# Low-rank up-projections with value and remainder stacked in one tile: two matmuls for three, and one for three

## The chip, the cores and the metric

The kernel runs on one core of one Trainium2 chip. The metric is the device time of one execution in microseconds (us): the median of the runs of a kernel. Engine names are those of the profile: PE (TensorE matmul), DVE (VectorE), ACT (ScalarE), POOL (GpSimd), SP (the queue that issues most DMAs).

## The reference

One encoder layer is applied to two batches of 512 tokens with width 1024. It has two branches on the normalised input, a recurrent one (RWKV7, run in both directions) and an attention one (MLA), then a gated feed-forward block. The part that the change touches feeds the recurrence: the decays, the rates and the output gate each come from a low-rank product.

```python
DECAY_LORA = 64; ICLR_LORA = 64; GATE_LORA = 160; A_WIDTH = 512
def decay(lora, up, base):
    wl = -jax.nn.softplus(-(base + jnp.tanh(lora) @ up)) - 0.5
    return jnp.exp(-jnp.exp(wl))
def iclr(lora, up, base):
    return jax.nn.sigmoid(base + lora @ up)
wf, wb = decay(pwf, w2[0], w0[0]), decay(pwb, w2[1], w0[1])   # forward, backward
af, ab = iclr(paf, a2[0], a0[0]), iclr(pab, a2[1], a0[1])
g = jax.nn.sigmoid(pg) @ g2
```

So four products have an inner size of 64, and the gate has one of 160.

## The kernel before

All large products keep float32 accuracy with a rounded matmul type: every operand is split into a rounded value "hi" and a remainder "lo" (`split`: ACT casts, DVE subtracts), and `mm3` adds three matmuls, hi by hi, hi by lo and lo by hi, into one PSUM tile.

The program has these stages. First the two inputs are normalised and transposed. Then `lora_phase` projects the input onto the low-rank columns (`proj` of tiles 4, 5, 6 and 3: "pj_w", "pj_a", "pj_g", "pj_x", 48 matmuls each of 512 columns, or their equal in halves), shifts them in time (`shifted`), applies tanh, and splits the results: `lw` (both decays: rows 0 to 63 forward, 64 to 127 backward), `la` (both rates), `lg` (128 of the gate's 160 rows) and `lx` (its last 32, in rows 64 to 95). After that a loop over four pairs of heads p and two batches b makes 40 PSUM tiles: four tiles "lu" (i = 0, 1 decays, 2, 3 rates) and one tile "lug" (the gate). A "lu" tile takes one `mm3`; its weights `w2` are zero in the 64 rows of the other direction. ACT applies tanh to it (tile "lut"), POOL scales it, and a DMA stores it to DRAM (`rwkv_in`). A "lug" tile takes two `mm3`, DVE copies it, and a DMA stores it. The PSUM tiles of this loop rotate over two banks (tag "mg"), the "lut" tiles over four buffers.

A scheduler of the framework sets each engine's order in this stage from its own time estimates, so that matmuls of later projections ("pj_rkv", "pj_mla") stand between the "lu" groups as long as there are any. From the next stage on (`drive`) the order of PE is written by the program: six threads (the recurrence's `state`, its `post`, `merge` and `prep`, the filler projections with the attention, and `combine`) are taken in turn by a model of PE time, in which the constants `L1`, `L2`, `L3`, `YS`, `YQ`, `YK` are the delays after which a thread may go on. `YS` stands ahead of a unit's recurrence, `L2` inside it; `YQ` and `YK` stand behind the query and key projections of the attention. The order of the other engines there is again the scheduler's. In the attention, "sc" are the scores of one block of queries, "mx" their maxima, "pr" the softmax (ACT exponential, DVE scaling), "pt" its transpose on PE, "pT" the copy of it by ACT, and "pav" the product with the values.

The feed-forward block and its down projection ("dx", "dy" in 2x2 blocks with split operands "dA", "dB", "dS", "dT") end the program.

Of the kernel before, what the change touches and what calls it, by code (L numbers as in the profile page):

```python
# [11 lines left out]
F32R = mybir.dt.float32r  # L12
# [6 lines left out]
P = 128  # L19
NB = 2  # L20
S = 512
# [18 lines left out]
ALAG = 2  # L40
NSTART = 27
L1 = 0.7
L2 = 0.9
L3 = 1.0
TL = 40
SLACK = 1.4
# [18 lines left out]
YO1 = 1.3  # L65
YO2 = 2.11
YO3 = 3.44
YS = 0.5
YQ = 2.6
YK = 1.4  # L70
OFFS = 200000, 150000, 120000, 100000, 0, 0
JP = NFF // 2
NRH = 10
# [31 lines left out]
def trunk(ctx, tc, outs, x, w_in, w2, g2, w_uq, w_ukk, w_ukv, w_oab, w_out, w_gu, w_down,  # L105
          cols, fng, ident, te, to, mask2, reset, blk64, blk2):
    nc = tc.nc
    out_p, out_s = outs

    def pool(stack, name, bufs=1, **kw):  # L110
        return stack.enter_context(tc.tile_pool(name=name, bufs=bufs, reuse_waits="tile", **kw))
# [11 lines left out]
    def mm(out, lhsT, rhs, start=True, stop=True, **kw):  # L123
        n = math.prod(rhs.shape[1:]) * (1 if rhs.dtype == F32R else 4) / 2400
        pin(nc.tensor.matmul(out, lhsT, rhs, start=start, stop=stop, **kw), n if out.shape[0] > 64 else n / 2)  # L125
# [5 lines left out]
    def split(hi, lo, src, eng=None):  # L131
        nc.scalar.copy(hi, src)  # L132
        (eng or nc.vector).tensor_sub(lo, src, hi)  # L133

    def mm3(out, whi, wlo, xhi, xlo, start=True, stop=True, **kw):
        mm(out, whi, xhi, start=start, stop=False, **kw)
        yield 0
        mm(out, whi, xlo, start=False, stop=False, **kw)
        yield 0
        mm(out, wlo, xhi, start=False, stop=stop, **kw)  # L140
        yield 0
# [88 lines left out]
    def mg(name):  # L230
        return psf.tile([P, S], F32, tag="mg", bufs=2, name=name)
# [52 lines left out]
    def proj(ti, name):  # L284
        res = [pf(f"pj_{name}{b}") for b in range(NB)]
        wt = []
        for q in range(2):
            raw = wp.tile([P, 4 * P], F32, tag="wraw", bufs=2, name=f"wraw_{name}{q}")
            nc.sync.dma_start(raw, w_in[ti][:, q * 512:(q + 1) * 512])
            hi = wp.tile([P, 4 * P], F32R, tag="whi", bufs=2, name=f"whi_{name}{q}")  # L290
            lo = wp.tile([P, 4 * P], F32R, tag="wlo", bufs=2, name=f"wlo_{name}{q}")
            split(hi, lo, raw)
            wt.append((hi, lo))
        n = 2 if ti in HALVES else 1
        for b in range(NB):
            for q in range(n):
                qs = slice(q * S // n, (q + 1) * S // n)
                for k in range(KD):
                    hi, lo = wt[k // 4]
                    ks = slice(k % 4 * P, (k % 4 + 1) * P)  # L300
                    yield from mm3(res[b][:, qs], hi[:, ks], lo[:, ks], h_hi[b][:, k, qs], h_lo[b][:, k, qs],
                                   start=(k == 0), stop=(k == KD - 1))
        return res

    def sh(name):
        return wp.tile([P, S], F32, tag="sh", bufs=2, name=name)
# [97 lines left out]
    def lora_phase():  # L404
        with ExitStack() as sl:
            lp = pool(sl, "lora")
            lw = [[lp.tile([P, S], F32R, name=f"lw{b}{i}") for i in range(2)] for b in range(NB)]
            la = [[lp.tile([P, S], F32R, name=f"la{b}{i}") for i in range(2)] for b in range(NB)]
            lg = [[lp.tile([P, S], F32R, name=f"lg{b}{i}") for i in range(2)] for b in range(NB)]
            lx = [[lp.tile([P, S], F32R, name=f"lx{b}{i}") for i in range(2)] for b in range(NB)]  # L410
            tosb = lp.tile([64, S], F32, name="tosb")
            nc.sync.dma_start(tosb, to[0:64])
            for b, ps in enumerate((yield from proj(4, "w"))):
                t = sh(f"shw{b}")
                shifted(t, ps, T_W)
                nc.scalar.activation(t, t, AF.Tanh)
                split(*lw[b], t)
            for b, ps in enumerate((yield from proj(5, "a"))):
                t = sh(f"sha{b}")
                shifted(t, ps, T_A)  # L420
                split(*la[b], t)
            for b, ps in enumerate((yield from proj(6, "g"))):
                t = sh(f"shg{b}")
                shifted(t, ps, T_G)
                nc.scalar.activation(t, t, AF.Tanh, scale=0.5)
                nc.vector.tensor_scalar(t, t, 0.5, 0.5, op0=ALU.mult, op1=ALU.add)
                split(*lg[b], t)
            for b, ps in enumerate((yield from proj(3, "x"))):
                t = sh(f"shx{b}")
                nc.vector.memset(t, 0.0)  # L430
                r = slice(64, 96)
                shifted(t, ps, T_X, r)
                nc.scalar.activation(t[r], t[r], AF.Tanh, scale=0.5)
                nc.vector.tensor_scalar(t[r], t[r], 0.5, 0.5, op0=ALU.mult, op1=ALU.add)
                split(*lx[b], t)
                ta, tb = sh(f"kra{b}")[0:32], sh(f"krb{b}")[0:32]
                nc.vector.tensor_mul(ta, ps[0:32], tosb[0:32])
                nc.vector.tensor_mul(tb, ps[32:64], tosb[32:64])
                nc.vector.tensor_add(ta, ta, tb)
                nc.sync.dma_start(kr_d[b][0:32], ta)  # L440
                nc.sync.dma_start(kr_d[b][32:64], ta)
            w2hi = lp.tile([P, 4, S], F32R, name="w2hi")
            w2lo = lp.tile([P, 4, S], F32R, name="w2lo")
            g2hi = lp.tile([P, 2, S], F32R, name="g2hi")
            g2lo = lp.tile([P, 2, S], F32R, name="g2lo")
            for i in range(4):
                t = lp.tile([P, S], F32, tag="raw", bufs=2, name=f"w2raw{i}")
                nc.sync.dma_start(t, w2[i])
                split(w2hi[:, i], w2lo[:, i], t)
            for i in range(2):  # L450
                t = lp.tile([P, S], F32, tag="raw", bufs=2, name=f"g2raw{i}")
                nc.sync.dma_start(t, g2[i])
                split(g2hi[:, i], g2lo[:, i], t)
            for p in range(NPAIR):
                for b in range(NB):
                    sl_p = slice(p * P, (p + 1) * P)
                    for i in range(4):
                        src = lw if i < 2 else la
                        ps = mg(f"lu{b}{p}{i}")
                        yield from mm3(ps, w2hi[:, i, sl_p], w2lo[:, i, sl_p], src[b][0], src[b][1])  # L460
                        t = lp.tile([P, S], F32, tag="lut", bufs=4, name=f"lut{b}{p}{i}")
                        dst = t[:, ::-1] if i % 2 else t
                        hcol = half[:, i * 4 + p:i * 4 + p + 1]
                        nc.scalar.activation(dst, ps, AF.Tanh, scale=0.5, bias=hcol)  # L464
                        f = -0.5 * KAPPA if i < 2 else 0.5
                        nc.gpsimd.tensor_scalar(t, t, f, f, op0=ALU.mult, op1=ALU.add)  # L466
                        nc.sync.dma_start(rwkv_in[b][p][:, 3 + i], t)
                    ps = mg(f"lug{b}{p}")
                    yield from mm3(ps, g2hi[:, 0, sl_p], g2lo[:, 0, sl_p], lg[b][0], lg[b][1], stop=False)
                    yield from mm3(ps, g2hi[:, 1, sl_p], g2lo[:, 1, sl_p], lx[b][0], lx[b][1], start=False)  # L470
                    t = lp.tile([P, S], F32, tag="lut", bufs=4, name=f"lugt{b}{p}")
                    nc.vector.tensor_copy(t, ps)
                    nc.sync.dma_start(rwkv_in[b][p][:, 7], t)
        yield from rkv_tiles(0)
# [53 lines left out]
    def attn_q(ap, b, hd, qn, tab):  # L528
# [13 lines left out]
        split(qh, ql, qf, QLE(nc))  # L542
        return qh, ql, pe["now"] + pe["cost"] + YQ

    def attention(ap, meanwhile):
# [45 lines left out]
        for (b, hd), (b1, hd1) in zip(heads, heads[1:] + [(NB, 0)]):  # L591
# [7 lines left out]
            for qb in range(4):  # L599
# [12 lines left out]
                if b1 < NB:  # L612
# [4 lines left out]
                    if qb == 3 and e == 1:  # L617
                        if hd1 == 0:
                            kt = attn_kr(ap, b1)
                        attn_kt(kt, kps)  # L620
                        q = (q[0], q[1], max(q[2], pe["now"] + YK))
                while len(pending) > ALAG:
# [63 lines left out]
    class Unit:  # L686
# [195 lines left out]
        def state(self):  # L882
# [20 lines left out]
            for c in range(NCH):  # L903
# [25 lines left out]
                nc.vector.tensor_copy(svb[HB, :, c], s2[HB])  # L929
                yield L2  # L930
                if not last:
# [49 lines left out]
    def state_thread():  # L981
        for i in range(NU):
            yield has("merge", i)
            yield has("prep", i)
            yield YS
            yield from units[i].state()
# [622 lines left out]
def layout(i):  # L1609
    f = np.float32  # L1610
    a = {k: np.asarray(v) for k, v in i.items()}
    r = {}
# [18 lines left out]
    r["w_in"] = wt.reshape(len(cols), P, KD * P)  # L1631
    w2 = np.zeros((4, P, 512), f)
    for d in range(2):
        w2[d, d * 64:(d + 1) * 64] = a["decay_w2"][0, d]
        w2[2 + d, d * 64:(d + 1) * 64] = a["iclr_a2"][0, d]
    r["w2"] = w2
    g2 = np.zeros((2, P, 512), f)
    g2[0] = a["gate_g2"][0, :128]
    g2[1, 64:96] = a["gate_g2"][0, 128:]
    r["g2"] = g2  # L1640
    uq = a["w_uq"][0].reshape(2, P, 8, 96)
    even = np.concatenate([np.arange(96), 80 + np.arange(16), 64 + np.arange(16)])
# [76 lines left out]
```

## Time and profile before

| | |
|---|---|
| median of 3 runs | 1831.26 us (1829.73 to 1834.43) |
| profiled execution | 1833.27 us |
| its span, first to last instruction | 1831.4 us |
| mean granted PE clock | 0.979 |
| PE busy | 1725.9 us (94%) |
| DVE, ACT, POOL busy | 1116.1, 771.4, 640.4 us |

The profiled execution stands 2.0 us above the median, of which the span leaves out 1.9 us. A busy share says how long an engine had an instruction under way; since matmuls overlap, the length of a PE stretch is read from the distance between starts, not from the duration of a matmul. The chain of work that ended last is followed back from the end of the program; a wait in it moves the end, a wait outside does not.

### The profile page before, as it was taken

To read this page: it belongs to the slowest core of one execution; us is meant where nothing else is said; L and a number is where in the kernel's file an instruction comes from. 1 tells how busy PE (TensorE), PEld (TensorE's weight loads), DVE (VectorE), ACT (ScalarE), POOL (GpSimd) and SP (SyncE) were. 2 spreads that over 40 slices of the span, in tenths; PEclk is the share of its full clock that TensorE was granted. 3 is DMA by queue.
4 is the path that set the end of the run, shared out by engine and by line. 5 is a ranking of instruction groups with operands and counts; after the bars stand their busy time and mean duration, and the time that the engine had idled before them with its cause. 6 is when DMAs were issued, how large, how long until landed. Compare 5 with 4: busy or idle time off the path is not lost.

```text
span 1831.4 us, 30995 instructions
## 1 busy us (share of the span) xinstructions
PE 1725.9 (94%) x11676; PEld 1357.8 (74%) x11676; DVE 1116.1 (61%) x1957; ACT 771.4 (42%) x1496; POOL 640.4 (35%) x992
## 2 busy tenths in 40 slices
PE   6999989999999998899989999699999999989997
PEld 6887767777777775565656979578888888868886
DVE  6633555635355455877776556865655556588757
ACT  5434343333344335666663233333333333335445
POOL 3012345363644627161012124853434333200006
PEclk8999989999999998999999999899999999999999
DMA  4354433434333334212067651022222222374442
GB/s 165 121 175 162 124 106 89 119 80 126 106 107 117 84 109 117 60 34 58 28 240 229 194 175 35 24 81 93 97 96 90 93 81 90 100 270 128 131 139 92
DMA packets 185333, 208.97 MB, mean 114 GB/s; under 512 B 102816, under 2 KB 114464, under 8 KB 185184
## 3 DMA queue, kind: packets, MB, share of 16 engines
q1 hardware_dynamic: 184320, 205.48, 35.9%
q8 instruction: 92, 1.51, 0.3%
q10 hardware_dynamic: 720, 0.98, 0.2%
q0 software_dynamic: 144, 0.52, 0.1%
q14 instruction: 57, 0.47, 0.1%
HBM read 147.70 MB, written 59.24 MB: 113 GB/s over the span
## 4 chain that ended last, share of the span: by engine, by line
PE 67%; DVE 10%; DMA 8%; POOL 7%; issue 4%; ACT 3%; SPq 1%; POOLq 0%; DVEq 0%; ACTq 0%
PE pgC L125 10%; PE pgB L125 6%; PE pgA L125 6%; PE pj_gt L125 6%; PE pj_rkv L125 5%; PE dx L125 5%; PE dy L125 3%; POOL el L841 2%; POOL lt L839 2%; PE pab L125 2%; PE s L125 2%; PE pav L125 2%; PE pj_mla L125 2%; DMA wor<-in_w_out 2%; PE gx L125 2%
## 5 line engine op out<-in xcount | busy, mean ns | idle before, releaser
L839 POOL TENSOR_TENSOR lt<-lane,el 128x126 f32<-128x126 f32 (+22 forms) x248 | 95.6, 386 | 40.8 <-DMA lane<-nt_d 22.3
L841 POOL TENSOR_TENSOR el<-el,lt 128x126 f32<-128x126 f32 (+22 forms) x248 | 98.5, 397 | 19.1
L125 PE MATMUL pab<-yo,wab 128*128 128x512 f32 x384 | 94.8, 400 | 8.3 <-ACT yo L132 3.7
L125 PE MATMUL pj_gt<-h_lo,whi_gt 128*128 128x512 f32 x240 | 99.5, 415 | 0.0
L125 PE MATMUL pj_gt<-h_hi,whi_gt 128*128 128x512 f32 x240 | 99.0, 413 | 0.0
L125 PE MATMUL pj_gt<-h_hi,wlo_gt 128*128 128x512 f32 x240 | 98.4, 410 | 0.5 <-DVE wlo_gt L133 0.5
L125 PE MATMUL pwo<-woh,m 128*128 128x256 f32 x512 | 93.6, 283 | 0.0
L125 PEld LDWEIGHTS pab<-yo,wab 128*128 128x128 f32 x384 | 71.0, 190 | 29.1 <-DVE wab L133 4.8
L1209 POOL TENSOR_TENSOR s<-uraw 128x512 f32<-128x512 f32 x22 | 29.2, 1328 | 153.3 <-DMA uraw<-in_w_gu 153.3
L125 PEld LDWEIGHTS pwo<-woh,m 128*128 128x128 f32 x512 | 80.3, 192 | 0.3
L125 PE MATMUL pj_rkv<-h_hi,whi_rkv 128*128 128x512 f32 x192 | 79.4, 414 | 0.0
L125 PE MATMUL pj_rkv<-h_hi,wlo_rkv 128*128 128x512 f32 x192 | 79.0, 415 | 0.0
L125 PE MATMUL pj_rkv<-h_lo,whi_rkv 128*128 128x512 f32 x192 | 78.4, 409 | 0.0
L125 PE MATMUL pwo<-wol,m 128*128 128x256 f32 x256 | 72.4, 284 | 0.5 <-DVE wol L133 0.5
L1588 POOL TENSOR_TENSOR x<-x,dp 128x512 f32<-128x512 f32 x4 | 6.3, 1590 | 176.9 <-DVE x L1587 176.9
L1277 DVE TENSOR_TENSOR p<-p,pgC 128x512 f32<-128x512 f32 x22 | 15.1, 687 | 86.9 <-PE pgC L125 86.9
L1056 POOL TENSOR_TENSOR g<-g 128x512 f32<-128x512 f32 x16 | 24.5, 1533 | 97.1 <-DVE g L1054 85.9
L928 ACT COPY sva<-s 64x128 f32<-64x128 f32 x64 | 16.5, 257 | 95.6 <-PE s L125 86.3
L466 POOL TENSOR_SCALAR lut<-lut 128x512 f32<-128x512 f32 x32 | 20.5, 642 | 98.4 <-ACT lut L464 98.1
L929 DVE COPY svb<-s 64x128 f32<-64x128 f32 x64 | 18.9, 295 | 57.6 <-ACT sva L928 34.8
L125 PEld LDWEIGHTS pj_gt<-h_hi,wlo_gt 128*128 128x128 f32 x240 | 45.1, 188 | 9.4 <-DVE wlo_gt L133 1.2
L125 PEld LDWEIGHTS pj_gt<-h_hi,whi_gt 128*128 128x128 f32 x240 | 45.1, 188 | 8.8
(1559 smaller groups left out, 5570.2 us busy)
## 6 DMA issues: line engine op xcount, KB each, us to landing
graw<-in_w_gu SPq DMA_DIRECT2D x22, 512.0 KB, 3.5
uraw<-in_w_gu SPq DMA_DIRECT2D x22, 512.0 KB, 3.5
a_d<-a SPq DMA_DIRECT2D x21, 512.0 KB, 3.2
w<-in_w_down SPq DMA_DIRECT2D x42, 256.0 KB, 4.3
x<-in_x SPq DMA_DIRECT2D x16, 512.0 KB, 7.8
rwkv_in<-lut SPq DMA_DIRECT2D x32, 256.0 KB, 2.0
gate_d<-gtt SPq DMA_DIRECT2D x32, 256.0 KB, 2.4
wab<-in_w_oab SPq DMA_DIRECT2D x32, 256.0 KB, 3.5
```

The costliest lines, as they stand in the source:

```text
L125: pin(nc.tensor.matmul(out, lhsT, rhs, start=start, stop=stop, **kw), n if out.shape[0] > 64 else n / 2)
L466: nc.gpsimd.tensor_scalar(t, t, f, f, op0=ALU.mult, op1=ALU.add)
L839: eng.tensor_mul(lv, lane[:, s, s + 1:].unsqueeze(1).to_broadcast([P, m_, n]), el[:, 0:m_, s].unsqueeze(2).to_broadcast([P, m_, n]))
L841: eng.tensor_add(ev, ev, lv)
L928: nc.scalar.copy(sva[HA, :, c], s2[HA])
L929: nc.vector.tensor_copy(svb[HB, :, c], s2[HB])
L1056: nc.gpsimd.tensor_add(g_[:, 0], g_[:, 0], g_[:, 1])
L1209: vg(ES[min(j, 1)]).tensor_add(s1, a21, a22)
L1277: nc.vector.tensor_add(p1, p1, x_)
L1588: nc.gpsimd.tensor_add(xs(1, t, 1), xs(1, t, 1), p5[t])
```

## The change

1. `lw` and `la`: for each direction one tile is made in which the 64 rows of this direction hold the rounded value, and the other 64 rows hold its remainder (`stacked`). The weights `w2` hold the direction's 64 rows twice. One matmul with the rounded weights then gives hi by hi and hi by lo at once, and a second one with the weights' remainder gives lo by (hi + lo). Each "lu" tile takes two matmuls.
2. `lx`: one tile per batch holds the last 32 gate rows three times, as value, value and remainder, and a tile `g2x` the weights as remainder, value, value, so that one matmul takes the place of three.
3. Three matmuls per "lug" tile for `lg` stay as they were.
4. The splitting takes more instructions of fewer rows: per `lw` or `la` tile two casts and two subtractions of 64 rows, per `lx` three casts and one subtraction of 32 rows.
5. Four delays of the PE model: `L2` 0.9 to 1.04, `YS` 0.5 to 0.41, `YQ` 2.6 to 2, `YK` 1.4 to 1.72.

```diff
-L2 = 0.9
+L2 = 1.04
-YS = 0.5
-YQ = 2.6
-YK = 1.4
+YS = 0.41
+YQ = 2
+YK = 1.72
...
+            top, bot = slice(0, 64), slice(64, 128)
+
+            def stacked(dst, t):
+                for d, (own, other) in enumerate(((top, bot), (bot, top))):
+                    nc.scalar.copy(dst[d][own], t[own])
+                    nc.vector.tensor_sub(dst[d][other], t[own], dst[d][own])
...
-                split(*lw[b], t)
+                stacked(lw[b], t)
...
-                split(*la[b], t)
+                stacked(la[b], t)
...
-                split(*lx[b], t)
+                for rows, own in ((slice(0, 32), slice(0, 32)), (r, r), (slice(32, 64), r)):
+                    nc.scalar.copy(lx[b][rows], t[own])
+                nc.vector.tensor_sub(lx[b][96:128], t[r], lx[b][r])
...
-                split(g2hi[:, i], g2lo[:, i], t)
+                if i == 0:
+                    split(g2hi, g2lo, t)
+                else:
+                    nc.scalar.copy(g2x[bot], t[bot])
+                    nc.scalar.copy(g2x[0:32], t[0:32])
+                    nc.vector.tensor_sub(g2x[32:64], t[64:96], g2x[64:96])
...
-                        yield from mm3(ps, w2hi[:, i, sl_p], w2lo[:, i, sl_p], src[b][0], src[b][1])
+                        mm(ps, w2hi[:, i, sl_p], src[b][i % 2], stop=False)
+                        yield 0
+                        mm(ps, w2lo[:, i, sl_p], src[b][i % 2], start=False)
+                        yield 0
...
-                    yield from mm3(ps, g2hi[:, 0, sl_p], g2lo[:, 0, sl_p], lg[b][0], lg[b][1], stop=False)
-                    yield from mm3(ps, g2hi[:, 1, sl_p], g2lo[:, 1, sl_p], lx[b][0], lx[b][1], start=False)
+                    yield from mm3(ps, g2hi[:, sl_p], g2lo[:, sl_p], lg[b][0], lg[b][1], stop=False)
+                    mm(ps, g2x[:, sl_p], lx[b], start=False)
+                    yield 0
...
-        w2[d, d * 64:(d + 1) * 64] = a["decay_w2"][0, d]
-        w2[2 + d, d * 64:(d + 1) * 64] = a["iclr_a2"][0, d]
+        w2[d] = np.tile(a["decay_w2"][0, d], (2, 1))
+        w2[2 + d] = np.tile(a["iclr_a2"][0, d], (2, 1))
...
-    g2[1, 64:96] = a["gate_g2"][0, 128:]
+    g2[1, 64:] = np.tile(a["gate_g2"][0, 128:], (2, 1))
```

In the built program PE has 48 rows of matmuls fewer (32 of "lu", 16 net of "lug"), DVE 4 instructions more, ACT 9 more (in 7 more rows); POOL's order is the same. Ahead of "lug02" (batch 0, pair 2), 28 of the 48 are taken out between projections; from its first row to the end of "lug13", with no projection between them, 20. Numbers in the names below: batch, pair, product; the number behind the underscore only tells tiles apart. PE, the tile "lu120" and its successor before:

```order
L125 MATMUL lu120_1007<-lw10_383,w2hi_769 128x512
L125 MATMUL lu120_1007<-lw11_384,w2hi_769 128x512
L125 MATMUL lu120_1007<-lw10_383,w2lo_770 128x512
L125 MATMUL lu121_1015<-lw10_383,w2hi_769 128x512
L125 MATMUL lu121_1015<-lw11_384,w2hi_769 128x512
L125 MATMUL lu121_1015<-lw10_383,w2lo_770 128x512
```

and PE at the same place with the change, with the end of "lug02" ahead of it:

```order
L125 MATMUL lug02_981<-lx0_393,g2x_783 128x512
L125 MATMUL lu120_989<-lw10_383,w2hi_779 128x512
L125 MATMUL lu120_989<-lw10_383,w2lo_780 128x512
L125 MATMUL lu121_996<-lw11_384,w2hi_779 128x512
L125 MATMUL lu121_996<-lw11_384,w2lo_780 128x512
```

Nothing moves against its neighbours there; a row is gone from each tile, and the two directions now read tiles of their own.

The second place is ACT ahead of the second "rkv" projection, whose rounded weights are "whi_rkv010". "kt000" reads "a000", a rate of the first unit that has gone through DRAM: "lut002", POOL, a store, and a load. ACT before, from "lut002" on:

```order
L464 ACTIVATE lut002_817<-lu002_813,half_65 128x512
L132 CAST lg00_389<-shg0_659 128x512
L464 ACTIVATE lut003_825<-lu003_821,half_65 128x512
L425 ACTIVATE shg1_667<-shg1_667 128x512
L132 CAST lg10_391<-shg1_667 128x512
L743 ACTIVATE kt000_1577<-a000_1567,oka_66,col_60 128x512
```

and ACT with the change:

```order
L482 ACTIVATE lut002_826<-lu002_823,half_65 128x512
L443 CAST lx0_393<-shx0_743 32x512 x2
L482 ACTIVATE lut003_833<-lu003_830,half_65 128x512
L309 ACTIVATE shx1_761<-pj_x1_682,c0_64 32x512
L443 CAST lx1_394<-shx1_761 32x512
L762 ACTIVATE kt000_1541<-a000_1531,oka_66,col_60 128x512
L440 ACTIVATE shx1_761<-shx1_761 32x512
L482 ACTIVATE lut100_848<-lu100_845,half_65 128x512
L443 CAST lx1_394<-shx1_761 32x512 x2
L132 CAST whi_rkv010_1174<-wraw_rkv010_1172 128x512
```

"lu002" and "lu003" now stand on PE behind the whole of "pj_x" (before: ahead of it), so "lut002" and "kt000" come later; before, "whi_rkv010" stood ten rows behind "kt000", now four.

The third place is DVE in the attention, where "pr013" (batch 0, head 1, last block of queries) is scaled beside the preparation of the last recurrence unit ("kra130", "bt130", "kt130", "c113", "bt131", "kt131"). DVE before:

```order
L605 TENSOR_REDUCE mx020_8332<-sc020_8315 128x1
L961 TENSOR_TENSOR os12_8145<-os12_8145,rbp_gn12_8324 128x512
L758 TENSOR_TENSOR kra130_8426<-nkk13_8283,pp130_8394 128x8x64
L759 TENSOR_TENSOR kra130_8426<-rkv13_8006,pp130_8394 128x8x64
L609 RECIPROCAL mx013_8264<-mx013_8264 128x1
L741 TENSOR_TENSOR bt130_8398<-bt130_8398,c013_8389 128x512
L745 TENSOR_TENSOR kt130_8401<-kt130_8401,c013_8389 128x512
L606 TENSOR_SCALAR mx020_8332<-mx020_8332 128x1
L740 SCALAR_TENSOR_TENSOR bt131_8414<-nkk13_8283,a131_8407 128x512
L605 TENSOR_REDUCE mx021_8349<-sc021_8345 128x1
L744 TENSOR_TENSOR kt131_8417<-kt131_8417,rkv13_8006 128x512
L734 SCALAR_TENSOR_TENSOR c113_8405<-rst_361,c113_8405 128x512
```

with "pr013" as the next row; and with the change:

```order
L624 TENSOR_REDUCE mx020_8296<-sc020_8279 128x1
L628 RECIPROCAL mx013_8228<-mx013_8228 128x1
L980 TENSOR_TENSOR os12_8111<-os12_8111,rbp_gn12_8288 128x512
L759 SCALAR_TENSOR_TENSOR bt131_8378<-nkk13_8247,a131_8371 128x512
L624 TENSOR_REDUCE mx021_8313<-sc021_8309 128x1
L763 TENSOR_TENSOR kt131_8381<-kt131_8381,rkv13_7972 128x512
L625 TENSOR_SCALAR mx020_8296<-mx020_8296 128x1
L629 TENSOR_SCALAR pr013_8231<-pr013_8231,mx013_8228 128x512
L777 TENSOR_TENSOR kra130_8390<-nkk13_8247,pp130_8358 128x8x64
L778 TENSOR_TENSOR kra130_8390<-rkv13_7972,pp130_8358 128x8x64
L760 TENSOR_TENSOR bt130_8362<-bt130_8362,c013_8353 128x512
L764 TENSOR_TENSOR kt130_8365<-kt130_8365,c013_8353 128x512
```

Five instructions, the two "kra130", "bt130", "kt130" and the scan "c113", stand behind "pr013" instead of ahead of it; a little earlier "kt011", which frees a PSUM tile, has passed "bo13" and the scan "c013". On ACT, eight instructions stand between the exponential of "pr013" and the copy "pT01" that follows the transpose of "pr013" and "kt131": "kt131" first, then "pp130", "pT01" of the block before, "c013", "os12", "e030", the exponential of "pr020" and the cast "wqh05".

Elsewhere the order differs in small ways: the matmuls "sc00x", "qps01" and "vps00" at the attention's start stand up to six rows earlier between the recurrence's rows, and in the down projection "dx" and "dy" groups and their DVE splits trade places by a few rows.

More of the change, by code (lines that the diff above doesn't have):

```diff
@@ L409, in lora_phase @@
             lg = [[lp.tile([P, S], F32R, name=f"lg{b}{i}") for i in range(2)] for b in range(NB)]
-            lx = [[lp.tile([P, S], F32R, name=f"lx{b}{i}") for i in range(2)] for b in range(NB)]
+            lx = [lp.tile([P, S], F32R, name=f"lx{b}") for b in range(NB)]
             tosb = lp.tile([64, S], F32, name="tosb")
@@ L443, in lora_phase @@
             w2lo = lp.tile([P, 4, S], F32R, name="w2lo")
-            g2hi = lp.tile([P, 2, S], F32R, name="g2hi")
-            g2lo = lp.tile([P, 2, S], F32R, name="g2lo")
+            g2hi = lp.tile([P, S], F32R, name="g2hi")
+            g2lo = lp.tile([P, S], F32R, name="g2lo")
+            g2x = lp.tile([P, S], F32R, name="g2x")
             for i in range(4):
```

## The prediction

> **What bounds the kernel now.** I read the page's first part, then the chain, then the stretches of the stage that changes, then its instructions in order of time.
>
> ```profile
> PE 1725.9 (94%) x11676; PEld 1357.8 (74%) x11676; DVE 1116.1 (61%) x1957; ACT 771.4 (42%) x1496; POOL 640.4 (35%) x992
> PE 67%; DVE 10%; DMA 8%; POOL 7%; issue 4%; ACT 3%; SPq 1%; POOLq 0%; DVEq 0%; ACTq 0%
> ```
>
> PE is busy nearly all the time and is two thirds of the chain, so matmuls taken away can shorten the program, if PE is the bound where they stand. The stretches say where it is (start and end, length, then busy time and instructions of PE, PEld, DVE, ACT and POOL, the granted clock, the DMA share, GB/s):
>
> ```profile
> 53.00:141.65 88.65, 88.65 (x390) 72.78 (x388) 40.55 (x62) 39.25 (x64) 13.03 (x20) 1.00 0.46 149
> 141.65:158.00 16.35, 15.50 (x61) 10.42 (x60) 2.08 (x3) 8.27 (x12) 7.26 (x12) 1.00 0.55 210
> ```
>
> The first stretch runs from the first "lu" matmul to the start of "lug02". PE never waits there: 390 matmuls in 88.65 us, 0.2273 us each, since the scheduler has projections to put between the "lu" tiles. The second is what is left of the loop when they have run out: "lug02" to the end of "lug13", 60 matmuls, which would take 13.6 us at 0.2273 and take 16.35. Here PE waits for the two PSUM banks. Its rhythm in order of time (start, duration, engine, line):
>
> ```profile
> 141.65 0.62 PE L125 MATMUL lug<-lg,g2hi 128*128 128x512 f32 x2
> 142.80 0.40 PE L125 MATMUL lug<-lx,g2lo 128*128 128x512 f32 x1
> 143.28 0.69 DVE L472 COPY lugt<-lug 128x512 f32<-128x512 f32 x1 [5.81 <-PE lug L125]
> 143.49 0.39 PE L125 MATMUL lu<-lw,w2lo 128*128 128x512 f32 x1
> 143.96 0.69 ACT L464 ACTIVATE lut<-lu,half 128x512 f32<-128x512 f32 x1 [5.07 <-issue]
> 144.03 0.73 PE L125 MATMUL lu<-lw,w2hi 128*128 128x512 f32 x2 [0.16 <-DVE lugt L472]
> 144.84 0.63 PE L125 MATMUL lu<-la,w2hi 128*128 128x512 f32 x2
> 146.63 0.64 PE L125 MATMUL lug<-lg,g2hi 128*128 128x512 f32 x2
> 156.60 0.64 PE L125 MATMUL lug<-lg,g2hi 128*128 128x512 f32 x2
> ```
>
> One group of five tiles takes 4.98 us (141.65 to 146.63; three of them end at 156.60), against 4.09 us of matmuls.
>
> **The change part by part.** First the 28 matmuls taken out of the dense stretch: 28 x 0.2273 = 6.4 us, on the path, as PE is the bound there. [...] The trace's 0.2273 is used.
>
> Second, the tail. A bank is held from the first matmul into it until ACT has read it. From the rows: the last matmul's start to ACT's start 0.47 us (143.49 to 143.96), ACT 0.69, and 0.19 until the next matmul there (144.65 to 144.84); for "lug" 0.48, DVE 0.69 and 0.06 (142.80, 143.28, 143.97, 144.03). Two banks alternate. With three and six matmuls these give 4.98 us a group, as measured. With two and four, from "lug" at 0: "lu" i = 0 starts at 0.91 in the other bank, ACT reads it from 1.61 to 2.30; i = 1 at 1.91; i = 2 at 2.49, but ACT is busy with i = 1 until 3.30; i = 3 at 3.49; the next "lug" at 4.18. So ACT and the banks bound it, not PE's 2.73 us. A second bound are the four "lut" buffers:
>
> ```profile
> L464 ACT ACTIVATE lut<-lu,half x32: 670/688/698, 56.5 to 156.8; 128x512 f32<-128x512 f32 x32
> L466 POOL TENSOR_SCALAR lut<-lut x32: 617/620/910, 57.3 to 157.6; 128x512 f32<-128x512 f32 x32
> DMA to landing us min/median/max: 2.0/2.0/5.9
> ```
>
> A buffer is held for 0.69 + 0.62 + 2.0 us and some 0.1 of issue, 3.4 us; five tiles over four buffers, the "lugt" one shorter by POOL's time, need 4.1 to 4.2 us a group too. Walking through both bounds together I get 4.17 and 4.34 in turn, 4.25 on the mean. The tail is three groups and one "lug": saved 3 x (4.98 - 4.25) + 2 x 0.23 = 2.7 us. The ends: 2.9 with the banks alone, 0.5 if a landing takes 2.6 us, at which the buffers ask for the old 5 us.
>
> Third, the added splits. An instruction of half the rows costs about as much as one of all:
>
> ```profile
> 54.92 0.62 ACT L132 CAST la<-sha 128x512 fp32r<-128x512 f32 x1
> 744.27 0.57 ACT L525 CAST kt<-kps 64x512 fp32r<-64x512 f32 x1
> 55.66 0.69 DVE L133 TENSOR_TENSOR la<-sha,la 128x512 fp32r<-128x512 f32 x1
> 746.26 0.67 DVE L526 TENSOR_TENSOR kt<-kps,kt 64x512 fp32r<-64x512 f32 x1
> ```
>
> So ACT gets 9 x 0.6 = 5.4 us more and DVE 4 x 0.67 = 2.7 us, at 39.25 and 40.55 us busy of 88.65: hidden, as long as no split of a weight comes late. The nearest risk is the second place of the order: "kt000" waits for a rate that goes through DRAM, and ACT's queue waits with it.
>
> ```profile
> 66.04 0.67 ACT L464 ACTIVATE lut<-lu,half 128x512 f32<-128x512 f32 x1
> 72.53 0.81 ACT L743 ACTIVATE kt<-a,oka,col 128x512 f32<-128x512 f32 x1 [2.62 <-DMA a<-rwkv_in]
> ```
>
> From "lut002" to "kt000" it is 6.5 us. With the change "lu002" stands behind "pj_x", at about 75.3 (8 matmuls less ahead), so "lut002" at 76 and "kt000" at 82.5; four rows later, with 0.6 to 0.8 us each, "whi_rkv010" is ready at 86.5. PE comes to it 62 matmuls after "lu002", at 89.4. Three microseconds of slack: cost 0, with 0 to 2 as its ends.
>
> Fourth, the delays. Up to the attention PE's order is the same apart from the missing rows, so the recurrence just starts earlier by what the loop saves. The one reordering with a price that the trace shows is the third place:
>
> ```profile
> 750.69 0.66 PE L129 MATMUL pt<-idn,pr 128*128 128x128 f32 x4 [1.22 <-DVE kt L526]
> 754.47 0.40 PE L125 MATMUL qps<-lat,wql 128*128 128x512 f32 x1
> 758.79 1.12 PE L129 MATMUL pt<-idn,pr 128*128 128x128 f32 x4 [3.93 <-DVE pr L610]
> 760.83 5.59 PE L125 MATMUL pav<-pT,vt 128*64 128x512 f32 x14
> 752.81 0.68 DVE L758 TENSOR_TENSOR kra<-nkk,pp 128x512 f32<-128x512 f32 x1
> 757.14 1.22 DVE L734 TENSOR_TENSOR_SCAN c<-rst,c 128x512 f32<-128x512 f32 x1
> 758.27 0.46 DVE L610 TENSOR_SCALAR pr<-pr,mx 128x512 f32<-128x512 f32 x1
> 752.93 0.82 ACT L743 ACTIVATE kt<-a,oka,col 128x512 f32<-128x512 f32 x1 [0.60 <-DMA a<-rwkv_in]
> 760.10 0.58 ACT L554 COPY pT<-pt 128x512 f32<-128x512 f32 x1
> ```
>
> PE stands for 3.93 us until "pr013" is scaled, and 1.22 us until "kt011" has freed a bank. With the change four instructions of 0.6 us and the scan of 1.2, 3.6 us in all, stand behind "pr013", and "kt011" is ahead of "bo13" and the scan. So PE would wait up to 5.1 us less. What is late next is the copy "pT01", which "pav" needs: on ACT it now follows "kt131" (waiting for its load until 751.5 to 752.9) by 5 us of work (0.82 + 0.63 + 0.58 + 0.63 + 0.80 + 0.36 + 0.88 + 0.40), so it starts at 756.6 to 758.0 in place of 760.10. I take the middle, 3.0 us (ends 0 and 5.1). The delayed "kra130" is needed by "gx" only at 769:
>
> ```profile
> 769.85 1.02 PE gx L125 x16
> ```
>
> The shifts at the attention's start and in the down projection go at 0, with 2 us either way: in the latter PE has no wait, and all its matmuls stay.
>
> ```profile
> 1640.00:1680.00 40.00, 40.00 (x178) 32.97 (x177) 37.49 (x63) 21.46 (x40) 0.00 (x0) 1.00 0.44 139
> ```
>
> Sum: 6.4 + 2.7 + 3.0 = 12.1 us. On the profiled execution's own 1833.27 us that gives 1821.2; against the median, 2.0 us lower, 1819.2, which is my forecast.
>
> **The rivals.** (a) The loop's 9.1 us come, the attention's 3.0 do not, because ACT's copy or another split takes over the wait at "pav": 1822.2. For it: the ACT queue above is long and full of waits of its own; against it: even its late end leaves 2.1 us.
>
> (b) The clock falls in the tail. Where PE has gaps, this trace shows a lower granted clock:
>
> ```profile
> 720.00:760.00 40.00, 32.57 (x273) 23.42 (x275) 31.95 (x76) 26.97 (x61) 12.21 (x28) 0.93 0.28 75
> 1160.00:1200.00 40.00, 23.38 (x79) 17.29 (x78) 37.22 (x33) 14.35 (x26) 32.57 (x21) 0.79 0.11 33
> 28.11 0.41 PE L125 MATMUL pj_w<-h_lo,whi_w 128*128 128x256 f32 x1
> 28.32 0.41 PE L125 MATMUL pj_w<-h_hi,wlo_w 128*128 128x256 f32 x1
> ```
>
> PE's matmuls would fill 2.73 of 4.25 us, 64%, between the 81% of the first row and the 58% of the second by the looser count of busy time. At the low clock 256 columns take 0.21 us, so 512 take 0.42, and a group's matmuls 5.1: the tail would save nothing, and the time be 1822. Against it: the gaps are at most 0.5 us, many times shorter than those in that stretch of 58%. [...]
>
> (c) A weight's split comes late in the dense stretch (the queue behind "kt000"): 1 to 3 us given back, about 1821 to 1822.
>
> (d) The gain is lost later and the time stays within 0.3% (5.5 us, about what a measurement of this kernel can tell): the loop's end is not followed by anything tied to a fixed time, but 12 us may shrink below 5.5 if the attention loses 2 and the tail saves little: 1826.
>
> (e) Slower: in the down projection DVE is full, and "dA_7l" comes later in its queue.
>
> ```profile
> 1643.78 0.68 DVE L133 TENSOR_TENSOR dA_7l<-araw,dA_7h 128x512 fp32r<-128x512 f32 x1
> 1647.14 0.39 PE L125 MATMUL dx<-dB_7h,dA_7l 128*128 128x512 f32 x1
> ```
>
> It is ready at 1644.5 and needed at 1647.1: 2.7 us, four places of 0.6. To reach 1837 a split would have to come 33 places late (2.7 + 12.1 + 5.5 us); the order shows four, and PE's use moves back too.
>
> **How the numbers follow.** Forecast 0.52, (a) 0.25, (b) 0.06, (c) 0.08, (d) 0.07, (e) 0.02. Faster by over 0.3%: the first four, 0.91; same 0.07; slower 0.02. The range: with all good ends 6.4 + 2.9 + 5.1 and 2 of the small shifts, 16.4 us, 1814.9, rounded down for the scatter of the runs to 1814; with the tail at 0.5, the attention at 0 and 1 lost on the way, 5.9, 1825.4. I give 1814 to 1825.5.
>
> **What would show it.** Right: the stretch from the first "lu" to "lug02" shorter by 6.4 us without waits of PE; "lug" to "lug" 4.2 to 4.4 us; ACT rather than PE named as what ends the gaps; no 3.93 us wait of "pt"; "pav" earlier than the loop's gain alone explains. Wrong: a wait of "pj_rkv" for a split, a tail still at 5 us, a clock under 1.00 there, or a new wait in "pav" or "dx".

## The result, and the profile after

The changed kernel takes 1819.78 us (median of six runs, 1816.87 to 1823.36) against 1832.01 us of the kernel before (six runs): ratio 0.9935, 95% interval 0.9921 to 0.9949. A second series of six runs on another occasion gave 1821.82 us against 1829.04 us (ratio 0.9956, interval 0.9941 to 0.9971). The medians put the gain at 12.2 us in the first series and at 7.2 in the second, the two intervals together at 5.3 to 14.5; the forecast was 12.1. One run of old_L2 took 1937.16 us at a mean granted clock of 0.837, its eleven others 1823.95 to 1831.55 us at 0.973 to 0.982; it is left out of its median below. The profiled execution took 1819.82 us, span 1818.0.

The page's first part and the shares of its chain, for the changed kernel:

```profile
PE 1713.7 (94%) x11628; PEld 1347.4 (74%) x11628; DVE 1119.9 (62%) x1961; ACT 779.0 (43%) x1505; POOL 643.3 (35%) x992
PE 67%; DVE 8%; DMA 8%; POOL 7%; issue 5%; ACT 3%; SPq 1%; POOLq 0%; DVEq 0%; ACTq 0%
```

PE is 12.2 us less busy, and no share of the chain moves by more than 2 points. The stretches, in the columns explained before: the dense part of the loop, its tail, the attention's start (last "pj_gtl" matmul to first "pav"), the output projection (last "pav" to last "pwo") and the down projection (first "dy" to the end):

```profile
53.59:135.38 81.79, 81.79 (x359) 67.20 (x358) 42.26 (x63) 44.09 (x71) 12.11 (x20) 1.00 0.45 155
135.38:151.47 16.09, 11.70 (x41) 6.43 (x40) 2.08 (x3) 7.87 (x12) 7.26 (x13) 1.00 0.61 233
691.60:744.40 52.80, 40.93 (x366) 29.22 (x361) 39.66 (x90) 35.02 (x80) 23.69 (x50) 0.88 0.38 112
948.90:1136.10 187.20, 183.72 (x1180) 163.65 (x1176) 113.90 (x181) 65.38 (x110) 53.34 (x40) 1.00 0.48 154
1591.40:1818.00 226.60, 210.68 (x900) 171.80 (x900) 170.08 (x266) 104.69 (x196) 32.52 (x25) 0.97 0.45 150
```

The same of before, but for the tail, which the prediction shows:

```profile
53.42:141.65 88.23, 88.23 (x388) 72.44 (x386) 40.22 (x61) 39.25 (x64) 13.03 (x20) 1.00 0.46 150
703.80:760.80 57.00, 42.36 (x363) 29.99 (x361) 42.40 (x97) 37.66 (x84) 26.66 (x55) 0.89 0.36 105
965.20:1155.60 190.40, 184.01 (x1179) 163.72 (x1176) 114.83 (x181) 64.82 (x110) 51.57 (x40) 1.00 0.47 151
1610.50:1831.40 220.90, 207.24 (x900) 169.55 (x900) 168.95 (x266) 103.93 (x196) 32.51 (x25) 0.98 0.46 155
```

The first stretch has no wait of PE, as forecast: counted from the first "lu" matmul, which here starts at 53.59 and before at 53.42 (not at the 53.00 from which the prediction's row counts), it fell from 88.2 to 81.8 us, 6.4. The tail is 16.09 long, against 16.35: the 2.7 us forecast there did not come. The attention's start gained 4.2 us, where 3.0 were forecast. The output projection gained 3.2 and the down projection lost 5.7, and for both nothing was forecast. So the total came out close to the forecast, but not by its sum.

The tail in order of time shows a new wait. "lug" starts every 4.07, then 5.45 and 5.53 us:

```profile
135.38 0.62 PE L125 MATMUL lug<-lg,g2hi 128*128 128x512 f32 x2
139.45 0.73 PE L125 MATMUL lug<-lg,g2hi 128*128 128x512 f32 x2
144.90 0.72 PE L125 MATMUL lug<-lg,g2hi 128*128 128x512 f32 x2 [0.21 <-ACT lut L482]
146.75 0.69 ACT L482 ACTIVATE lut<-lu,half 128x512 f32<-128x512 f32 x1 [1.33 <-DMA rwkv_in<-lut]
149.11 1.27 ACT L482 ACTIVATE lut<-lu,half 128x512 f32<-128x512 f32 x2 [1.66 <-DMA rwkv_in<-lut]
150.43 0.73 PE L125 MATMUL lug<-lg,g2hi 128*128 128x512 f32 x2
```

ACT waits 1.33 and 1.66 us for stores of "lut", for a free one of its four buffers, and PE behind it. The landings of the whole loop now have a median of 2.6 us in place of 2.0. In the tail itself, 13 of the 14 stores of before landed in 1.96 to 2.04 us; now 8 of 15 take 2.5 to 3.4. The row for "lut" in the whole loop:

```profile
DMA to landing us min/median/max: 2.0/2.6/5.8
```

### The profile page after: what moved, and what is told of

It reads as the page before. It is cut to its first block, busy times and chain, and to the rows that moved or that the text cites. A ratio compares the mean times of both kernels' runs of the same rounds, so it can differ in the third digit from the quotient of the medians.

```text
span 1818.0 us, 30918 instructions
## 1 busy us (share of the span) xinstructions
PE 1713.7 (94%) x11628; PEld 1347.4 (74%) x11628; DVE 1119.9 (62%) x1961; ACT 779.0 (43%) x1505; POOL 643.3 (35%) x992
## 4 chain that ended last, share of the span: by engine, by line
PE 67%; DVE 8%; DMA 8%; POOL 7%; issue 5%; ACT 3%; SPq 1%; POOLq 0%; DVEq 0%; ACTq 0%
PE pgC L125 10%; PE pj_gt L125 8%; PE pgB L125 6%; PE pgA L125 6%; PE dx L125 5%; PE pj_rkv L125 4%; PE pab L125 3%; PE dy L125 3%; PE s L125 2%; POOL el L860 2%; POOL lt L858 2%; PE pav L125 2%; PE sc L125 2%; DMA wor<-in_w_out 2%; PE gx L125 2%
## 5 line engine op out<-in xcount | busy, mean ns | idle before, releaser
L947 ACT COPY sva<-s 64x128 f32<-64x128 f32 x64 | 16.6, 259 | 96.7 <-PE s L125 85.4
```

The source lines that it names most:

```text
L947: nc.scalar.copy(sva[HA, :, c], s2[HA])
```

## The experiments

Two theories at the outset. A: the stacking and the four delays each work in their own place, the first in the loop, the second in the attention; and the tail is held by the four "lut" buffers. B: only the earlier arrival counts, and the delays do nothing. Twelve runs followed; their medians (in us) and ratios:

| kernel | median | before beside it | ratio, 95% interval | profiled span |
|---|---|---|---|---|
| changed kernel, first series | 1819.78 | 1832.01 | 0.9935 (0.9921 to 0.9949) | 1818.0 |
| after_again, second series | 1821.82 | 1829.04 | 0.9956 (0.9941 to 0.9971) | 1820.8 |
| stack_only | 1828.88 | 1829.31 | 0.9987 (0.9974 to 1.0000) | 1819.3 |
| stack_again (one run) | 1826.45 | 1829.04 | none | 1824.7 |
| delays_only | 1830.36 | 1829.31 | 1.0000 (0.9987 to 1.0013) | 1825.0 |
| before_lut6 | 1829.63 | 1829.31 | 1.0004 (0.9991 to 1.0018) | 1828.5 |
| old_L2 (eleven runs) | 1825.65 | 1829.04 | 0.9987 (0.9975 to 0.9999) | 1826.7 |
| old_YQK | 1824.13 | 1829.04 | 0.9966 (0.9954 to 0.9977) | 1820.6 |
| lut6 | 1818.62 | 1829.31 | 0.9940 (0.9924 to 0.9957) | 1817.6 |
| lut6_again | 1819.07 | 1830.13 | 0.9948 (0.9930 to 0.9966) | 1813.1 |
| lut6_PL | 1821.39 | 1830.13 | 0.9953 (0.9937 to 0.9969) | 1819.4 |
| lut8 (one run) | 1822.71 | 1830.13 | none | 1820.9 |
| lut8_timed | 1818.19 | 1830.15 | 0.9938 (0.9921 to 0.9955) | 1816.6 |

From their traces, the length of each stage in us (worked out as the difference between the starts and ends of the matmuls named; where a kernel or an order has two traces, both; before_lut6 has before's order on PE, DVE, ACT, POOL and SP and stands as its second trace):

| from the last row's end to | before, before_lut6 | delays_only | stack_only, stack_again | old_L2 | old_YQK | changed, after_again | lut6, lut6_again | lut6_PL | lut8, lut8_timed |
|---|---|---|---|---|---|---|---|---|---|
| end of "lug13" (from first "lu") | 104.6, 104.9 | 104.6 | 97.8, 98.2 | 99.8 | 98.5 | 97.9, 98.2 | 96.5, 96.5 | 96.7 | 95.6, 95.6 |
| first "o" | 120.1, 116.7 | 115.4 | 114.5, 116.2 | 117.6 | 118.3 | 114.6, 115.9 | 115.0, 114.4 | 116.9 | 115.4, 116.4 |
| last "pj_rkv" | 75.4, 75.3 | 75.4 | 77.8, 76.7 | 77.8 | 76.9 | 77.7, 77.3 | 76.8, 76.6 | 76.6 | 78.5, 78.7 |
| last "pj_gtl" | 350.3, 348.3 | 349.1 | 346.6, 349.6 | 346.3 | 349.4 | 347.8, 349.6 | 347.3, 349.0 | 347.1 | 351.2, 347.4 |
| first "pav" | 57.0, 57.3 | 55.3 | 54.9, 54.6 | 52.1 | 55.5 | 52.8, 52.5 | 52.9, 51.9 | 51.4 | 51.7, 51.5 |
| last "pav" | 204.4, 203.0 | 203.9 | 203.9, 203.6 | 208.6 | 203.2 | 204.5, 205.4 | 206.5, 203.6 | 206.8 | 205.5, 206.1 |
| last "pwo" | 190.4, 192.6 | 189.3 | 188.4, 190.2 | 192.7 | 185.0 | 187.2, 186.5 | 186.9, 186.0 | 192.6 | 188.6, 187.3 |
| first "dy" | 454.9, 454.1 | 454.8 | 456.4, 455.3 | 454.8 | 454.1 | 455.3, 455.2 | 455.3, 454.1 | 454.8 | 454.1, 455.4 |
| end | 220.9, 222.8 | 224.0 | 225.0, 226.5 | 223.7 | 226.5 | 226.6, 226.8 | 226.7, 226.4 | 223.5 | 226.9, 224.0 |

**The two parts apart.** stack_only is the changed kernel with the old delays:

```
-L2 = 1.04   +L2 = 0.9
-YS = 0.41   +YS = 0.5
-YQ = 2      +YQ = 2.6
-YK = 1.72   +YK = 1.4
```

> The stacked rows with the four delays of the kernel before. Theory A (the two parts work by themselves): the loop of the low-rank products gives 6.7 us and the step from there to the first o tile some 3 us more, the attention's 4 us are gone: 1822 to 1825 us, and the two waits of pt of about 4 and 1 us at the attention's start are back. Rival B (the attention's gain comes from the earlier arrival, not from the delays): within 1 us of the changed kernel, 1819 to 1821, without those waits.

delays_only is the kernel before with the same four lines the other way round.

> The kernel before with the four new delays and nothing stacked. Theory A: 3 to 4 us faster than before, 1828 to 1829, first o tile and last pj_gt within 0.5 us of the kernel before, the 3.9 us wait of pt before pr013 gone. Rival B: no change, 1831 to 1833, or slower, since the delays were set for the earlier arrival.

Neither theory stands: the stacking alone gives 0 to 5 us by its interval, the delays alone no difference in time, and the two together 7 to 12 by their medians. In the trace of delays_only the two waits of "pt" are gone all the same, as theory A says, and the attention's start is 55.3 us in place of 57.0 and 57.3; yet its median is no lower than that of before. The loop's gain is there with the stacking (97.8 us in place of 104.6), so it must be lost later, at a place where the delays matter. stack_again was run for a second trace, since the first was of its fastest run:

> The stacked rows with the old delays again, for a second trace, since the first trace was of its fastest run of twelve (1821.1 us, median 1828.9). Theory A (the old delays make stalls of PE in the attention, and half-speed windows follow them): 1826 to 1831 us, at least 2 us more of PE waits than in the changed kernel between kps and the last pav, and windows of half speed there that add up to 7 us or more beyond the changed kernel's. Rival B: the loss lies outside the attention, in the loads of the output and down projections.

It shows neither more half speed nor lost microseconds between "kps" and the last "pav" beyond the two waits of "pt"; the row that differs is the next, from the last "pav" to the last "pwo": 188.4 and 190.2 against 187.2 and 186.5. Rival B of that expectation, outside the attention, holds for about half of what the traces show.

**Which delay.** after_again is the changed kernel once more, as a neighbour; old_L2 sets only L2 back to 0.9, old_YQK only YS, YQ and YK (YS alone moves no instruction).

> The changed kernel once more, beside the same runs of the kernel before as the next three. Theory A (the gain is tied to the order, not to one lucky trace): 1819 to 1821 us, 0.9925 to 0.9945 of before. Rival B (the first six runs were lucky): 1822 to 1826. In its trace the half-speed windows lie behind the same stalls of PE as in the first trace (the recurrence's start at about 179 us, kps at 695, the turn into the down projection at 1592 and 1612), but some are missing and others longer by 3.4 us.

> The changed kernel with L2 back at 0.9, the other three delays new. Theory A (L2, which places every step of the recurrence, carries the delays' part): 1825 to 1829 us, like the stacked rows with all old delays. Rival B (YQ and YK carry it): 1819 to 1821. Rival C (the four only fit together): 1823 or more here and with YS, YQ and YK old.

> The changed kernel with YS, YQ and YK back at their old values, L2 at 1.04. Theory A: 1819 to 1821 us. Rival B: 1825 to 1829. Rival C: 1823 or more. YS alone moves no instruction.

after_again lies at the border of its two theories. Of the parts, rival C fits best: old_L2 is 4.2 us above the changed kernel's median of all twelve runs (1821.4), old_YQK 2.7. The interval of old_L2 lies apart from that of after_again; that of old_YQK overlaps it, so its cost is likely and not shown by the times. The traces say where. With YQ and YK old, the attention's start is 55.5 us in place of 52.5, and the two waits of "pt" stand there as before (PE's waits from the last "pj_gtl" to the first "pav" in old_YQK: waiter, line, releaser, total us, times, longest):

```profile
PE kps L125 <- ACT wkh L132: 5.1, 1, 5.1
PE pt L129 <- DVE pr L629: 3.9, 1, 3.9
PE pt L129 <- DVE kt L545: 1.2, 1, 1.2
```

With L2 old, the attention's start is short (52.1) and the output projection long: 192.7 in place of 187.2 and 186.5. That stage knows two orders of SP's queue. In before, before_lut6, delays_only, stack_only, stack_again, old_L2 and lut6_PL it reads (loads between "wor001" and "wab061")

```
wab031 graw0 graw1 uraw0 wab030 wor002 wor003 g330 wab041 wab040 wor010 g340 wor011 wab051 wab050 wor012 g350 wor013
```

and in the changed kernel, after_again, old_YQK and all with more buffers but lut6_PL

```
graw0 graw1 wab031 uraw0 wor002 wab030 wor003 g330 wab041 wor010 wab040 wor011 g340 wab051 wor012 wab050 wor013 g350
```

The seven traces of the first order take 188.4 to 192.7 us in that stage, mean 190.9; the seven of the second 185.0 to 188.6, mean 186.8: 4.1 us. The two groups touch, and two of the first (old_L2 and lut6_PL) have 3.4 us at half PE speed there, which none of the second has. PE's waits in the first 45 us of the stage separate them better: 2.1 to 5.3 us with the first order, mean 3.7, and 0.4 to 1.6 with the second, mean 0.9. PE's own order in the stage is the same in both but for lut6_PL. The waits there, from the last "pav" on, in stack_only (949.5 to 995) and then in the changed kernel (948.9 to 990):

```profile
PE pab L125 <- DVE g L1073: 2.1, 2, 1.0
PE pab L125 <- DVE wab L133: 1.0, 2, 0.6
PE pab L125 <- ACT wab L132: 0.7, 1, 0.7
```

```profile
PE pab L125 <- DVE wab L133: 0.4, 1, 0.4
```

So PE waits 3.4 us less for "wab" and "g" there in this pair of traces, though later waits leave only 1.2 us of it in the length of the stage (188.4 and 187.2). That the order of the loads does it is read from the queue and from the waits of all fourteen traces; no run moved these loads alone. The second order came only with the stacking and the new L2 together, which would explain why the parts don't add up. The account is not complete: the medians put the stacking with the old delays 7.1 us above the changed kernel (1828.5, the median of stack_only and stack_again, against 1821.4). Of that their traces show 2.1 us at the attention's start and 2.4 in the output projection (4.1 by the means of the two groups); the rest is not located.

**The tail.** lut6 has six buffers in place of four, for "lut" and "lugt"; before_lut6 does that to the kernel before; lut8 has eight.

```
-t = lp.tile([P, S], F32, tag="lut", bufs=4, ...)
+t = lp.tile([P, S], F32, tag="lut", bufs=6, ...)
```

> The changed kernel with six buffers for lut and lugt in place of four. Theory A (in the tail the stores' landings hold the four buffers): the 3.0 us of ACT waiting for the stores of lut are gone, the groups of the tail take 4.2 us in place of 5.5, the stretch from lug02 to the end of lug13 falls from 16.1 to 13.5 us or somewhat more, and the program is 2 to 2.6 us faster, 1817 to 1818. Rival B (ACT and the two banks bound the tail): 16 us as now and no change. Rival C: the tail shrinks, but the next stage waits for the same stores and gives it back: 13.5 us in the tail, and less than 0.5 us at the first gx.

> The kernel before with six buffers for lut and lugt. Theory A (there the two banks bound the tail at 4.98 us a group): 16.3 us from lug02 to the end of lug13 and the same time, within 0.5 us. Rival B (the buffers bound it there as well): a group of 4.3 us, 2 us faster.

> The changed kernel with eight buffers for lut and lugt. Theory A (the tail with six is still held by buffers): its third group, 5.1 us with six, falls to 4.2, and lug02 to the end of lug13 to 13.6 us. Rival B (the rate at which the stores are issued and land holds it, whatever the number of buffers): the waits move, the stretch stays at 14 us or more.

The stretch from "lug02" to the end of "lug13" in lut6, then in lut8:

```profile
135.53:150.21 14.68, 11.49 (x42) 6.52 (x41) 2.08 (x3) 7.96 (x12) 7.56 (x13) 1.00 0.70 269
```

```profile
135.17:148.96 13.79, 11.37 (x41) 6.38 (x40) 2.08 (x3) 7.94 (x12) 7.19 (x13) 1.00 0.71 271
```

From 16.09 with four buffers to 14.7 with six and 13.8 with eight: the buffers hold the tail. With six it stays above the 13.5 us of theory A; with eight it is close to the 13.6 us that the prediction's 2.7 leave of 16.35. In lut8 the groups take 4.05, 4.18 and 4.52 us:

```profile
135.17 0.62 PE L125 MATMUL lug<-lg,g2hi 128*128 128x512 f32 x2
139.22 0.72 PE L125 MATMUL lug<-lg,g2hi 128*128 128x512 f32 x2
143.40 0.73 PE L125 MATMUL lug<-lg,g2hi 128*128 128x512 f32 x2
147.92 0.74 PE L125 MATMUL lug<-lg,g2hi 128*128 128x512 f32 x2
```

Why did the landings grow, when before's tail has the same stores? How densely the stores come is not enough to explain it. In lut8 five stores, issued from 138.22 to 141.30 us, landed in 2.0 to 2.3 us; in the changed kernel four, issued from 139.54 to 141.81 and no closer together, took 2.5 to 2.9. The queues and the stores (count, size, median landing), in lut8 from 138.2 to 142.4, then in the changed kernel from 139.5 to 142.5:

```profile
q1 hardware_dynamic: 657, 1.20, 74.0%
rwkv_in<-lut SPq DMA_DIRECT2D x4, 256.0 KB, 2.0
rwkv_in<-lugt SPq DMA_DIRECT2D x1, 256.0 KB, 2.3
```

```profile
q1 hardware_dynamic: 483, 0.89, 77.1%
q14 instruction: 2, 0.02, 1.9%
rwkv_in<-lut SPq DMA_DIRECT2D x3, 256.0 KB, 2.9
rwkv_in<-lugt SPq DMA_DIRECT2D x1, 256.0 KB, 2.5
```

The second has two packets of a queue that the profile lists as "instruction". Over all fourteen traces, the 86 stores of the tail with such a packet under way landed in 2.9 us at the median, the 121 others in 2.0. Each tail with the stacking has three such packets, each without it one. No run takes them away, so that they delay the stores is likely and not shown.

before_lut6 is unchanged there (104.9 against 104.6 for the loop) and in time: before the change the banks held it, as the prediction had it. Does the tail's gain reach the end?

> Eight buffers for lut and lugt again, now timed, since the first look (1822.7 us) had more half-speed windows than its neighbours. Theory A (the tail's 2.3 us, from 16.1 to 13.8, reach the end): 1817 to 1819 us, the lowest median of all kernels here, with 13.6 to 14 us from lug02 to the end of lug13. Rival B (they are eaten by the stalls behind it, which wait for loads, or are lost in the scatter of the windows): 1819.5 us or more.

1818.19 us, the lowest median of all, and lut6 and lut6_again 1818.6 and 1819.1, against 1819.8 and 1821.8 of the changed kernel: the right order and size, but the intervals of the ratios overlap, so a gain of 2 us at the end is likely and not shown.

**The down projection.** There PE's and SP's order has two forms as well: that of before, shared by before_lut6 and old_L2, and another in the rest. PL at 3.65 (when "pav" falls due in the planner's order) gives the form of before back, with the stacking and six buffers:

```
-PL = 3.5
+PL = 3.65
```

> The changed kernel with six buffers for lut and lugt once more, as the neighbour of the next kernel. Expected 1817 to 1820.5 us; in the trace the stretch from lug02 to the end of lug13 14.5 to 14.9 us, the output projection (last pav to last pwo) 186 to 188 us, and from the first dy matmul to the end 225 to 227 us.

> Six buffers for lut, and PL at 3.65 in place of 3.5. That moves a few dozen rows in the attention and the gates, and gives the down projection on PE and on SP's queue exactly the order that the kernel before has. Theory A (the changed kernel loses 2 to 4 us in the down projection by that order): from the first dy matmul to the end 222 to 224 us in place of 226.7, and 1814 to 1817 us. Rival B (the loss there is only where the half-speed windows happen to lie): 225 to 227 us in that stretch and the time of its neighbour within 1.5 us. Rival C (the moved rows at the end of the attention take it back): the stretch from the last pav to the last pwo back at 190 us, and no gain.

The stretch came out as theory A has it (223.5 us, lut6_again 226.4), and rival C as well: PL also turned the output projection's queue back to the first order, 192.6 us in place of 186.0, so there is no gain in all. PE's waits at the start of the down projection, in the changed kernel (1586 to 1665), then in lut6_PL (1590 to 1670):

```profile
PE dy L125 <- ACT dS_0h L132: 3.5, 1, 3.5
PE dx L125 <- ACT dA_4h L132: 2.9, 1, 2.9
PE dx L125 <- ACT dA_3h L132: 1.7, 1, 1.7
PE dx L125 <- ACT dA_8h L132: 1.3, 1, 1.3
```

```profile
PE dy L125 <- ACT dS_0h L132: 3.5, 1, 3.5
PE dx L125 <- ACT dA_4h L132: 2.9, 1, 2.9
PE dx L125 <- ACT dA_3h L132: 1.8, 1, 1.8
```

The order accounts for the wait for "dA_8h", 1.3 us: all ten traces of the other form have it, and none of the four with the form of before. The rest of the 2.9 us is a stretch of 3.4 us at half PE speed near the end, which lut6_again has and lut6_PL has not; lut8_timed, too, is at 224.0 us with the changed kernel's order. So rival B holds for about half. The last section shows behind what such stretches came.

## Why the prediction was right, and where it was not

The time was forecast as 1819.2 us and measured as 1819.8 and 1821.8. Its steps:

- Dense stretch, 6.4 us: right, 88.2 to 81.8 us, no wait of PE. "kt000" began at 84.06 us, where 82.5 was worked out; the splits behind it were in time, and rival (c) did not come.
- Tail, 2.7 us: the step that failed. It measured 0.3. The two bounds were the right ones, but the term for a landing in the buffers' hold was too small: the prediction took 2.0 us, which fits before's tail, and with the change 8 of 15 stores there took 2.5 to 3.4, so it came out even below the lower end, 0.5 "if a landing takes 2.6 us". With the change the four buffers, not ACT and the banks, set the pace; eight buffers brought 2.3 of the missing 2.4 us. What lengthens the landings stays open; the packets of the "instruction" queues are the likely cause (a median of 2.9 us with one under way, 2.0 without).
- Added splits, 0: right; they wait for nobody on PE's path.
- The attention's start, 3.0 us: right in mechanism. As a size it was the middle between 0 and 5.1, and by the prediction's own rows the upper end is 3.6 + 1.2 = 4.8. old_YQK against the changed kernel, 55.5 to 52.8 and 52.5, is 2.7 to 3.0. The waits of 3.9 and 1.2 us are gone, and part of it comes back as a new wait at the bank of "qps" (1.62 us, for the copy "pT" behind a "kt" that waits for its load), not at "pav", so rival (a) is right about ACT's copy and wrong about its size:

```profile
736.89 0.60 PE L129 MATMUL pt<-idn,pr 128*128 128x128 f32 x4
739.82 0.74 PE L125 MATMUL qps<-lat,wqh 128*128 128x512 f32 x2 [1.62 <-ACT pT L573]
742.38 1.12 PE L129 MATMUL pt<-idn,pr 128*128 128x128 f32 x4
744.42 1.98 PE L125 MATMUL pav<-pT,vt 128*64 128x512 f32 x4
```

- "The shifts at the attention's start and in the down projection go at 0": wrong for the second, even with its 2 us either way: 221.9 us became 226.7, on the mean of two traces each. That "PE has no wait" there was read from 40 us of it; in the whole stage PE of before waits 5.8 us, 2.2 of them for "dA_4h". The new order costs 1.3 us by the wait for "dA_8h", and more by half-speed stretches. Rival (e) named DVE's split "dA_7l"; it was ACT's rounded copy "dA_8h".
- What the prediction left out altogether: the output projection's queue, 4.1 us gained, and the stage up to the last "pj_rkv", 1.2 us or more lost in every kernel with the stacking (75.4 to 77.5 on the mean of the two traces), where PE in the two traces of the changed kernel waits 2.3 and 1.9 us for "svb" and "z" of the recurrence and before only 0.5.

Added up by the rows of the table, on the mean of the two traces of each kernel, the places that the prediction priced give 11.2 us: 6.7 in the loop (9.1 forecast) and 4.5 at the attention's start (3.0 forecast). The other seven rows, set at 0, come to -0.6: 4.6 gained in the output projection, 4.8 lost in the down projection, 3.1 gained up to the first "o" (an estimated 2.6 of it because less of these traces runs at half speed: there 6.8 us in the changed kernel's first trace, 17.1 in that of before), and the rest small. The sum, 10.6, lies within the measured 7 to 12. That it is near 12.1 is in part luck: the attention gave more than its term, and two large shifts that the prediction did not see nearly cancel.

Rival (b), the clock in the tail, is half right. The first trace shows 1.00 there; that of after_again has one half-speed stretch, in which 3.4 us hold 8 matmuls in place of 15:

```profile
143.50:146.90 3.40, 3.40 (x8) 2.14 (x8) 0.00 (x0) 1.68 (x3) 2.25 (x4) 0.50 0.50 193
```

Four of the six traces with the stacking and four buffers have one there (after_again, stack_again, old_L2, old_YQK), and none of the five with more buffers. It is cheap here, where PE waits anyway: the loop takes 98.2 us in after_again against 97.9, and at most 99.8 (old_L2). In after_again PE is busy for 1.84 of the 3.41 us before that stretch. Waits like these don't settle it alone: in the first trace PE is busy for 2.00 and 1.80 us in two such pieces of the tail (141.19 to 144.60 and 148.01 to 151.43), and no half speed follows.

## What to carry to other kernels

When matmuls are taken out of a loop, the next bound can be the number of buffers behind it (here the tail took 16.1 us with four and 13.8 with eight): cost a buffer's hold with the long landings that the trace shows, not with the median alone, and test it with a run that has more buffers. Where a scheduler sets the order, a change at one end can flip the order of a queue hundreds of microseconds later (here 4.1 us gained in one stage, 1.3 lost in another): look at each difference on the DMA queue, and compare stage by stage before crediting the edit. Take such an account over more than one trace of a kernel. A time that agrees with the forecast proves no term of it.

## What the runs showed of the hardware

Executions of one kernel differ by several microseconds (before: 1822.4 to 1834.9 us in 29 runs). Stretches of half PE speed that fall differently are a part of it: by their mean granted clocks, 0.976 to 0.982, these runs have an estimated 66 to 88 us at half speed, and more of it goes with a longer time, but loosely (correlation 0.40). In the 14 traces the granted clock changes on a grid of 3.41 us that has no fixed phase to the program (its edges lie 0.19 us behind the first instruction in before's trace, 1.24 in the changed kernel's first). I counted PE's busy share in each piece of the grid at full speed (from the matmuls' records, from 30 us on, without the stage at 165 to 190 us): of 133 pieces under 0.44 busy, all were followed by half speed; of 176 between 0.44 and 0.7, 27; of over 6,600 above 0.7, none. The stage left out goes against it: 11 pieces over 0.7 busy by their records are followed by half speed there, beside matmuls of a single column ("lss"). So a wait of 2 to 3 us cost, by an estimate from these pieces, up to 1.7 us more for a piece at half speed (half of 3.41), or nothing, by where it lay on the grid. The wait for "dA_4h" shows both. In the changed kernel its 2.92 us lie in one piece, in before its 2.20 us lie across two (pieces of the grid; the column before the last two is the clock):

```profile
1608.90:1612.31 3.41, 0.49 (x3) 0.42 (x3) 3.41 (x7) 1.75 (x3) 0.00 (x0) 1.00 1.04 388
1612.31:1615.73 3.42, 3.42 (x10) 2.63 (x9) 2.37 (x4) 0.01 (x1) 0.00 (x0) 0.50 1.04 394
```

```profile
1624.94:1628.35 3.41, 2.83 (x13) 2.01 (x11) 3.41 (x7) 1.25 (x3) 0.00 (x0) 1.00 1.05 396
1628.35:1631.77 3.42, 1.80 (x8) 1.48 (x9) 3.42 (x7) 1.25 (x3) 0.00 (x0) 1.00 1.05 391
1631.77:1635.18 3.41, 3.41 (x17) 2.81 (x16) 2.98 (x5) 1.21 (x3) 0.00 (x0) 1.00 1.04 393
```

Such stretches make single profiles poor witnesses for a few microseconds: before's trace has 10.2 us at half speed after the stall at 260 us, before_lut6's 3.4 us, and that alone is most of the 3.4 us between their second rows in the table. In the down projection's 5.7 us (the two first traces), PE's waits grew by 2.3 us, from 5.8 to 8.1, and the time at half speed by 6.1, from 8.5 to 14.6, which makes an estimate of 3.0. What part of them is order and what is luck is settled only for the 1.3 us at "dA_8h".
